# Four norm borders of a two-layer transformer kernel written out by hand, and modulation weights in buffers of their own

## The chip, the core and the metric

The kernel runs on one core of a Trainium2 chip. Its engines are TensorE (PE, matmuls and weight loads), VectorE (DVE), ScalarE (ACT), GpSimd (POOL) and the DMA queues, here SyncE's (SP). Each engine works through a queue of its own in order. The metric is the device time of one execution in microseconds (us), taken as the median of several runs; the profile is one execution of its own.

## The reference

Two layers of a diffusion transformer with d = 1024 work on 256 latent tokens and 256 context tokens. Each layer has three steps: an FFN, a mixer, an FFN. The mixer is a short convolution in layer 0 and grouped-query attention in layer 1. Each step is preceded by an RMS norm with a modulation, and followed by a gated residual addition. Shift, scale and gate (nine vectors a layer, for each of the two streams) are products of silu(c) with a weight matrix. Only the latent stream is returned, so the context drops out after attention of layer 1.

```python
def _rms(t, g):
    y = t * rsqrt(mean(t * t) + eps);  return y * g
def _modulate(t, g, shift, scale):
    return _rms(t, g) * (1 + scale) + shift
def _swiglu(h, w13, w2):
    gte, up = split(h @ w13);  return (silu(gte) * up) @ w2

mod = silu(c) @ mod_w[i] + mod_b[i]            # 3 x (shift, scale, gate)
lat = lat + 0.5 * gate0 * _swiglu(_modulate(lat, g0, shift0, scale0), w13[i, 0], w2[i, 0])
lat = lat + gate1 * mixer(_modulate(lat, g1, shift1, scale1))
lat = lat + 0.5 * gate2 * _swiglu(_modulate(lat, g2, shift2, scale2), w13[i, 1], w2[i, 1])
# the context (ctx, c_ctx) goes through the same steps as long as attention still reads it
```

Here FFN (l, 0) and FFN (l, 1) are the first and second FFN of layer l, and norm (l, j) is the norm ahead of step j.

## The kernel before

**Data.** Features lie on the 128 partitions, in eight "k tiles"; tokens lie along the free axis, 512 columns: 256 latent (stream s = 0) and 256 context (s = 1). `x[:, k, :]` is the residual. Every matmul operand is split into a high part, rounded to the matmul's type, and a low part, the rest (`split`, L110: the high part by ScalarE at L111, the low by VectorE at L112). A product is three matmuls (`mm3`, L131: high x high at L135, high weights x low data at L136, low weights x high data at L137).

**Weights.** `load_raw` (L105) loads 1 MB pages into three buffers with the tag `wr`; the halves of a page are split into `wh` and `wl`.

**FFN** (`ffn`, L689). The 22 tiles of hidden features go in two halves of eleven. In each half some tiles are computed as "plain" units (`w13_mm`: 48 matmuls, over all 512 columns or over the two streams apart), the others as `Pair` units by a Strassen form (`prod`: 84 matmuls of 256 columns, on sums of quarters of the weights, and on sums T1 to T4 of the blocks of h, which `Blocks.sums` makes). `PLAIN` says how many are plain. The pair loop is written out by hand under `manual_schedule` for TensorE, VectorE and ScalarE; elsewhere a scheduler orders the instructions. After eleven tiles, `project` (L495) multiplies by w2: eight tiles of output (m), each a sum over eleven tiles of hidden features. Its start takes in what is left of the last pair: `prev.seven` with the addition `p` (L675), and `last` with `four`, `gate`, `gate_parts`. The conv mixer's and attention's projections use `project` too, over eight tiles.

**Norm borders.** In the projection that ends a step, m = 6 and 7 are computed by streams (`late`): m = 6, 7 for s = 0, and then for s = 1. `finish` (L474) adds gate x product to the residual (L479); `tail_norm` (L429) then squares (L252), accumulates (L255), and, behind m = 7, queues the norm as closures in `pending`, which `flush` runs at chosen places in the code. The norm itself is `rms_sums` (matmuls with ones, L267; root on ScalarE, L272; reciprocal, L276), `rms_rows` (1/rms broadcast over the partitions into PSUM by matmul, L281), and for each k tile and stream: `scaled` (VectorE, x times scale times 1/rms, L289), then on ScalarE the addition of the shift into the high part (L299), on VectorE the low part (L300). A `Blocks` norm also keeps an unsplit copy `hr` (L343) for the sums T1 to T4. `ready` (L493) runs a Sqrt early, which brings ScalarE's function table. Four borders are such: norm (0,1) ahead of the conv mixer, (0,2) ahead of FFN (0,1), (1,0) ahead of FFN (1,0), (1,1) ahead of attention. I call them borders 1 to 4. In borders 1, 3 and 4 the projection sums eleven tiles, in border 2 eight.

**Modulation.** The modulation vectors are made by VectorE in 224 units `junk` (L155), each 128x1024 with its product and sum. Their weights come as 64 pages `modT` of 1 MB through the same `wr` buffers: `open_job` loads a page and queues its four units (or two), `tick(n)` spends n units at a place in the code, `ask_ahead` loads a page early, and `mod_ready` runs what is still missing when a vector is needed.

**The last stage** (L1534 and on) projects FFN (1,1) for the latents alone. For two output tiles at a time it loads three pages: two of `w2l` and one of `w2m`.

Of the kernel before, what the change touches and what calls it, by code (L numbers as in the profile page):

```python
# [24 lines left out]
PLAIN = {(0, 0): 8, (0, 1): 2, (1, 0): 2, (1, 1): NM}  # L25
# [16 lines left out]
def hybrid_kernel(ctx: ExitStack, tc: tile.TileContext, a: dict, out: bass.AP):  # L42
# [62 lines left out]
    def load_raw(src, n=2048):  # L105
        raw = wp.tile([P, 2048], F32, name=nm("wr"), tag="wr", bufs=3)
        nc.sync.dma_start(raw[:, :n], src)
        return raw

# [39 lines left out]
    def mod_unit(l, ch, pair, raw, j, v):  # L149

        mt = mod_tile(l, ch)
        kt = pair * 2 + j
        col = ch * KT + kt
        junk = mp.tile([P, D], BF16, name=nm("junk"), tag="junk", bufs=1)
        nc.vector.tensor_tensor_reduce(  # L155
            out=junk,
            in0=raw[:, j * D : j * D + D],
            in1=scbc[:, v, :],
            scale=1.0,
            scalar=modb[:, l, col : col + 1],  # L160
            op0=ALU.mult,
            op1=ALU.add,
            accum_out=mt[:, kt, v : v + 1],
        )
        done[l, ch] += 1
# [4 lines left out]
    def mod_job(l, ch, pair):  # L170
        mod_tile(l, ch)
        raw = load_raw(a["modT"][l, ch * 4 + pair])
        for j in range(2):
            for v in range(streams(l, ch)):
                mod_unit(l, ch, pair, raw, j, v)

    jobs = [(0, ch, p) for ch in range(2, 9) for p in range(4)]
    jobs += [(1, ch, p) for ch in range(9) for p in range(4)]
# [4 lines left out]
    def open_job():  # L183
        l, ch, pair = jobs.pop(0)
        mod_tile(l, ch)
        raw = load_raw(a["modT"][l, ch * 4 + pair])
        units.extend(
            (l, ch, pair, raw, j, v) for j in range(2) for v in range(streams(l, ch))
        )

    def next_unit():
        if not units:
            open_job()
        with tc.issue_after(begun[-1].ins):
            mod_unit(*units.pop(0))

    def ask_ahead():
        if not units and jobs:
            open_job()
# [59 lines left out]
    def rms_inv(s, parts):  # L259
        return rms_rows(*rms_sums(s, parts))  # L260

    def rms_sums(s, parts):

        pq = psmall("ss")
        for i in range(2):
            for n, t in enumerate(parts):
# [3 lines left out]
                )  # L270
        rs = tp.tile([P, 2], F32, name=nm("rs"), tag="rs")
        nc.scalar.activation(  # L272
            out=rs, in_=pq[:, S : S + 2], func=AF.Sqrt, scale=1.0 / D, bias=eps_t
        )
        ri = tp.tile([P, 2], F32, name=nm("ri"), tag="ri")
        nc.vector.reciprocal(ri, rs)  # L276
        return pq, ri
# [8 lines left out]

    def scaled(s, k, A, ri):
        t = tp.tile([P, S], F32, name=nm("t"), tag="t", bufs=3)
        nc.vector.scalar_tensor_tensor(  # L289
            out=t, in0=x[:, k, s * S : s * S + S], scalar=A[:, k, s : s + 1], in1=ri,  # L290
            op0=ALU.mult, op1=ALU.mult,
        )
        return t

    def norm_k(s, k, h, A, B, ri, keep=None):
        hh, hl = pick(h, k, s * S, s * S + S)
        t = scaled(s, k, A, ri)
        b = B[:, k, s : s + 1]
        nc.scalar.activation(out=hh, in_=t, func=AF.Identity, bias=b)  # L299
        nc.vector.scalar_tensor_tensor(  # L300
            out=hl, in0=t, scalar=b, in1=hh.bitcast(F32), op0=ALU.add, op1=ALU.subtract
        )
        if keep is not None:
            nc.scalar.activation(out=keep, in_=t, func=AF.Identity, bias=b)
# [14 lines left out]

    def pick(h, k, c0, c1):  # L320
        return h.at(k, c0, c1)

    class Blocks:
# [5 lines left out]
        def block(self, s, hf, A, B, ri, fine=False):  # L329
            raw = self.raw[hf, s] = hot("hr", F32)  # L330
            hi, lo = self.t["B", hf, s] = hot("bh"), hot("bl")
            for i in range(4):
                k = 4 * hf + i
                c = slice(i * S, i * S + S)
                t = scaled(s, k, A, ri)
                b = B[:, k, s : s + 1]
                if fine:
                    nc.scalar.activation(out=hi[:, c], in_=t, func=AF.Identity, bias=b)
                    nc.vector.scalar_tensor_tensor(
                        out=lo[:, c], in0=t, scalar=b, in1=hi[:, c].bitcast(F32),  # L340
                        op0=ALU.add, op1=ALU.subtract,
                    )
                nc.scalar.activation(out=raw[:, c], in_=t, func=AF.Identity, bias=b)  # L343
            if not fine:
                split(hi, lo, raw)

        def at(self, k, c0, c1):
            return self.blk(("B", k // 4, c0 // S), k % 4)

        def blk(self, key, k):  # L350
            return tuple(t[:, k * S : k * S + S] for t in self.t[key])

        def sums(self, n):
# [3 lines left out]
            tt = nc.vector.tensor_tensor  # L357

            def keep(key, src):
                hi, lo = self.t[key] = hot("th"), hot("tl")  # L360
                split(hi, lo, src)

            if n == 0:
                tt(out=b11, in0=b12, in1=b11, op=ALU.subtract)
                keep("T1", b11)
            elif n == 1:
                tt(out=b12, in0=b22, in1=b12, op=ALU.add)
                tt(out=b22, in0=b22, in1=b11, op=ALU.add)
                keep("T2", b22)
            else:  # L370
                tt(out=b21, in0=b21, in1=b22, op=ALU.subtract)
                keep("T3", b12)
                keep("T4", b21)
# [48 lines left out]
    pending = []  # L422

    def flush(n=9):
        while pending and n:
            pending.pop(0)()
            n -= 1

    def tail_norm(l, j, h):  # L429

        box = {}

        def tail(m, c0, c1):
            square_add(m, c0, c1)
            if m == KT - 1:
                if not box:
                    box["A"] = scale_of(l, j)
                    box["B"] = mod_ready(l, 3 * j)
                s = c0 // S

                def inv():
                    return rms_inv(s, (accs[s], accs[s, "last"]))

                def rest(part, ri):

                    if isinstance(h, Blocks):
                        h.block(s, part, box["A"], box["B"], ri, fine=s == 0 and part == 0)
                    else:
                        for k in range(4 * part, 4 * part + 4):
                            norm_k(s, k, h, box["A"], box["B"], ri)  # L450

                def both_parts():
                    ri = inv()
                    for part in range(2):
                        rest(part, ri)

                if s == 0:
                    keep = []

                    def one():  # L460
                        keep.append(inv())
                        rest(0, keep[0])

                    pending.append(one)
                    pending.append(lambda: rest(1, keep[0]))
                    if (l, j) == (1, 2):
                        flush()
                else:
                    flush()
                    pending.append(both_parts)  # L470

        return tail

    def finish(m, ps, c0, c1, gate, tail):  # L474
# [12 lines left out]
        if tail:  # L487
            tail(m, c0, c1)
# [6 lines left out]
    def project(ws, src, nk, gate, tail, tot, late, ev, between=()):  # L495

        def products(ps, w, ks, c0, c1):
            for k in ks:
                mm3(ps[:, : c1 - c0], w(k), src(k, c0, c1), k == 0, k == nk - 1)
# [12 lines left out]
        if between:  # L517
            products(p2[0], w2[0], range(nk // 2), 0, tot)
            between[0]()
            products(p2[0], w2[0], range(nk // 2, nk - 2), 0, tot)  # L520
            between[1]()
            products(p2[1], w2[1], range(nk - 2), 0, tot)
            for i in range(nf):
                products(p2[i], w2[i], (nk - 2,), 0, tot)
        else:
            for i in range(nf):
                products(p2[i], w2[i], range(nk - 1), 0, tot)
        for i in range(nf):
            products(p2[i], w2[i], (nk - 1,), 0, tot)
            finish(i, p2[i], 0, tot, gate, tail)  # L530
            tick(ev)

        for m in range(nf, KT - late):
            if tail and tot == S and m == KT - 2:
                ready()
            w = get(m)
            ps = psum("py")
            products(ps, w, range(nk), 0, tot)
            finish(m, ps, 0, tot, gate, tail)
            if m < (KT - late - 1 if tail else KT - 2):  # L540
                tick(ev)
        if late:

            wl = [get(m) for m in (6, 7)]
            if tail:
                ready()
            for s in range(2):
                for i in range(2):
                    ps = psum("py")
# [1271 lines left out]
```

## Time and profile before

| | us |
|---|---|
| runs | 1585.12 to 1589.19, median 1587.78 |
| profiled execution, own time | 1588.48 |
| its span | 1586.3 |
| mean granted clock of TensorE | 0.992 |
| TensorE busy | 1559.8 |
| VectorE busy | 1301.8 |
| ScalarE busy | 731.1 |

The profile names an instruction by its line, its engine, its operation and its tiles (out<-in, buffer numbers left out). A row of groups gives the count, the busy time in us and the mean in ns of one, then the idle time of the engine just before and what ended it. A row of windows gives a stretch of the span in us, its length, and for each engine busy time and number of instructions, then the clock granted to TensorE, the DMA share and GB/s. A row of the chain gives the start, the length and what ran; a row of the timeline the same with the idle time before. Matmuls overlap: a matmul of 256 columns is listed with 0.28 us, but the next one starts 0.12 us later. Vector and scalar instructions overlap by somewhat under 0.1 us.

### The profile page before, as it was taken

To read this page: it belongs to the slowest core of one execution; us is meant where nothing else is said; L and a number is where in the kernel's file an instruction comes from. 1 tells how busy PE (TensorE), PEld (TensorE's weight loads), DVE (VectorE), ACT (ScalarE), POOL (GpSimd) and SP (SyncE) were. 2 spreads that over 40 slices of the span, in tenths; PEclk is the share of its full clock that TensorE was granted. 3 is DMA by queue.
4 is the path that set the end of the run, shared out by engine and by line. 5 is a ranking of instruction groups with operands and counts; after the bars stand their busy time and mean duration, and the time that the engine had idled before them with its cause. 6 is when DMAs were issued, how large, how long until landed. Compare 5 with 4: busy or idle time off the path is not lost.

```text
span 1586.3 us, 25078 instructions
## 1 busy us (share of the span) xinstructions
PE 1559.8 (98%) x10264; PEld 1427.5 (90%) x10264; DVE 1301.8 (82%) x1949; ACT 731.1 (46%) x1189; POOL 34.2 (2%) x28
## 2 busy tenths in 40 slices
PE   8999999999999999999999999999999899999998
PEld 6789899988888899988999899988999789998887
DVE  5787889987988789987997889988997866788654
ACT  4524245524322365522554365523554255775543
POOL 0000000000000000000000000000000002420000
PEclk9999999999999999999999999999999999999999
DMA  9353533255455413345333613355344832256552
GB/s 369 125 201 127 186 127 133 96 185 184 160 187 184 159 55 107 125 172 195 107 133 107 225 54 127 109 192 171 133 160 153 287 127 98 85 194 253 186 195 97
DMA packets 42498, 248.73 MB, mean 157 GB/s; under 512 B 5648, under 2 KB 8208, under 8 KB 18960
## 3 DMA queue, kind: packets, MB, share of 16 engines
q1 hardware_dynamic: 41664, 246.97, 44.1%
q8 instruction: 80, 1.31, 0.3%
q14 instruction: 34, 0.28, 0.1%
q10 hardware_dynamic: 720, 0.17, 0.0%
HBM read 244.77 MB, written 1.05 MB: 155 GB/s over the span
## 4 chain that ended last, share of the span: by engine, by line
PE 84%; DVE 9%; DMA 3%; ACT 3%; issue 1%; POOL 0%; DVEq 0%; ACTq 0%; POOLq 0%
PE py L135 8%; PE py L136 8%; PE py L137 8%; PE p L135 5%; PE p L137 5%; PE p L136 5%; PE q L137 4%; PE py L1534 4%; PE q L135 4%; PE q L136 4%; PE pg L1534 3%; PE pu L1534 3%; DMA wr<-in_modT 2%; DVE wl L611 2%; DVE junk L155 2%; PE pv L137 1%
## 5 line engine op out<-in xcount | busy, mean ns | idle before, releaser
L111 ACT ACTIVATE wh<-wr 128x1024 fp32r<-128x1024 f32 (+1 forms) x228 | 209.1, 936 | 274.2 <-PE py L136 91.4
L155 DVE CUSTOM_DVE_ANT_0 junk<-wr,scbc,modb 128x1024 bf16<-128x1024 f32 x224 | 286.9, 1281 | 30.9 <-DMA wr<-in_modT 28.8
L112 DVE TENSOR_TENSOR wl<-wr,wh 128x1024 fp32r<-128x1024 f32 (+1 forms) x228 | 241.7, 1073 | 64.1 <-ACT wh L111 26.9
L135 PE MATMUL py<-gh,wh 128*128 128x512 f32 (+1 forms) x594 | 219.2, 369 | 4.4 <-ACT wh L111 4.4
L608 ACT ACTIVATE wh<-wr 128x1024 fp32r<-128x1024 f32 x162 | 166.3, 1056 | 115.6 <-DVE wr L631 80.4
L136 PE MATMUL py<-gl,wh 128*128 128x512 f32 (+1 forms) x594 | 218.5, 368 | 0.0
L137 PE MATMUL py<-gh,wl 128*128 128x512 f32 (+1 forms) x594 | 218.2, 367 | 0.0
L611 DVE TENSOR_TENSOR wl<-wr,wh 128x1024 fp32r<-128x1024 f32 x162 | 192.9, 1217 | 22.6 <-ACT wh L608 22.6
L135 PEld LDWEIGHTS py<-gh,wh 128*128 128x128 f32 x594 | 113.5, 191 | 22.1 <-ACT wh L111 4.6
L137 PEld LDWEIGHTS py<-gh,wl 128*128 128x128 f32 x594 | 113.3, 191 | 18.2
L136 PEld LDWEIGHTS py<-gl,wh 128*128 128x128 f32 x594 | 113.3, 191 | 17.5
L136 PE MATMUL p<-tl,wh 128*128 128x256 f32 x432 | 122.3, 283 | 0.0
L137 PE MATMUL p<-th,wl 128*128 128x256 f32 x432 | 122.3, 283 | 0.0
L135 PE MATMUL p<-th,wh 128*128 128x256 f32 x432 | 122.2, 283 | 0.0
L137 PE MATMUL q<-bh,wl 128*128 128x256 f32 x320 | 90.8, 284 | 1.2 <-DVE wl L611 1.2
L135 PE MATMUL q<-bh,wh 128*128 128x256 f32 x320 | 90.7, 283 | 0.5 <-ACT wh L608 0.5
L136 PE MATMUL q<-bl,wh 128*128 128x256 f32 x320 | 90.6, 283 | 0.0
L136 PEld LDWEIGHTS p<-tl,wh 128*128 128x128 f32 x432 | 82.9, 192 | 0.2
L135 PEld LDWEIGHTS p<-th,wh 128*128 128x128 f32 x432 | 82.9, 192 | 0.2
L137 PEld LDWEIGHTS p<-th,wl 128*128 128x128 f32 x432 | 82.9, 192 | 0.0
L626 DVE TENSOR_TENSOR wr<-wr 128x1024 f32<-128x1024 f32 x54 | 66.1, 1224 | 1.6
L137 PE MATMUL q<-th,wl 128*128 128x256 f32 x216 | 61.8, 286 | 1.2 <-DVE wl L611 1.2
(326 smaller groups left out, 4109.1 us busy)
## 6 DMA issues: line engine op xcount, KB each, us to landing
wr<-in_w SPq DMA_DIRECT2D x85, 1024.0 KB, 4.8
wr<-in_modT SPq DMA_DIRECT2D x64, 1024.0 KB, 4.8
wr<-in_w2h SPq DMA_DIRECT2D x48, 704.0 KB, 4.1
mr<-in_mod SPq DMA_DIRECT2D x16, 512.0 KB, 9.0
wr<-in_cw_cx SPq DMA_DIRECT2D x8, 1024.0 KB, 4.8
wr<-in_w2l SPq DMA_DIRECT2D x8, 1024.0 KB, 4.8
wr<-in_cw_b SPq DMA_DIRECT2D x4, 1024.0 KB, 5.0
wr<-in_cw_out SPq DMA_DIRECT2D x4, 1024.0 KB, 5.1
```

Of the source, the lines that this page charges most:

```text
L111: nc.scalar.activation(out=hi, in_=src, func=AF.Copy)
L112: nc.vector.tensor_tensor(out=lo, in0=src, in1=hi.bitcast(F32), op=ALU.subtract)
L135: nc.tensor.matmul(ps, wh, mh, start=first, stop=False, **kw)
L136: nc.tensor.matmul(ps, wh, ml, start=False, stop=False, **kw)
L137: nc.tensor.matmul(ps, wl, mh, start=False, stop=last, **kw)
L155: nc.vector.tensor_tensor_reduce(out=junk, in0=raw[:, j * D : j * D + D], in1=scbc[:, v, :], scale=1.0, scalar=modb[:, l, col : col + 1], ...
L608: nc.scalar.activation(out=self.shaped(g, 0), in_=self.part(g), func=AF.Copy)
L611: nc.vector.tensor_tensor(out=self.shaped(g, 1), in0=self.part(g), in1=self.shaped(g, 0).bitcast(F32), op=ALU.subtract,)
L626: tt(out=by_two(raw[:, :1024]), in0=a21.unsqueeze(1).to_broadcast([P, 2, T2]), in1=by_two(raw)[:, :, :T2], op=ALU.subtract,)
L1534: nc.tensor.matmul(p[:, :n], w(j, k)[part], m(k)[:, :n], start=not part and k == 0, stop=part == 1 and k == nk - 1, skip_group_check=True,)
```

## The change

- Weight pages get two `wr` buffers in place of three. Modulation weights get two buffers `wm` of their own, each half as large, and are loaded in 128 halves of 512 KB; `ask_ahead` keeps two halves in hand and is called around each unit.
- FFN (0,1) and FFN (1,0), which begin at borders 2 and 3, have three plain units and eight pairs in the first half, in place of two and nine.
- The norm at borders 1 to 4 is a class `Border`. ScalarE makes x times scale (`scaled`) into `hr`, for k tiles 0 to 3 from m = 4 on, for 4 and 5 at the opening, and for 6 and 7 behind each square; when 1/rms is there, VectorE multiplies four k tiles at once (`mult`, 128x1024); `hi` (ScalarE) and `lo` (VectorE) split each k tile with its shift, and `shift` adds it in place for the block sums.
- The opening of each border (`open_border`: the four blocks of m = 6 and 7, the norm of s = 0 and the first weight splits) and the start of the next stage are written out for TensorE, VectorE and ScalarE. `part_mm` orders the matmuls by part (high x high, low weights, low data), so that they begin on the high parts of four k tiles. Modulation vectors of the norm are made ready when `Border` is made, at m = 4.
- `Halves` is a weight page whose two halves are split when asked; `Post` is the plain unit's silu, gate and split, step by step; `Blocks.sub`, `hi`, `lo` replace `Blocks.sums`.

```diff
-PLAIN = {(0, 0): 8, (0, 1): 2, (1, 0): 2, (1, 1): NM}
+PLAIN = {(0, 0): 8, (0, 1): 3, (1, 0): 3, (1, 1): NM}
...
-        raw = wp.tile([P, 2048], F32, name=nm("wr"), tag="wr", bufs=3)
+        raw = wp.tile([P, 2048], F32, name=nm("wr"), tag="wr", bufs=2)
...
+    def mod_raw():
+        return wp.tile([P, D], F32, name=nm("wm"), tag="wm", bufs=2)
...
+    def ask_ahead():
+        while jobs and len({u[2] for u in units}) < 2:
+            l, ch, kt = jobs.pop(0)
+            mod_tile(l, ch)
+            raw = mod_raw()
+            src = a["modT"][l, ch * 4 + kt // 2]
+            nc.sync.dma_start(raw, src[:, kt % 2 * D : kt % 2 * D + D])
+            units.extend((l, ch, kt, raw, v) for v in range(streams(l, ch)))
...
+    class Border:
+        def scaled(self, k, s):
+            nc.scalar.activation(
+                out=self.part(k, s), in_=x[:, k, s * S : s * S + S], func=AF.Identity,
+                scale=self.A[:, k, s : s + 1],
+            )
...
+        def mult(self, hf, s):
+            t = self.raw[hf, s].rearrange("p (k t) -> p k t", k=4)
+            nc.vector.tensor_tensor(
+                out=t, in0=t, in1=self.ss[s][:, :S].unsqueeze(1).to_broadcast([P, 4, S]),
+                op=ALU.mult,
+            )
...
+    def open_border(bd, v, early=False):
+        short = bd.nk == KT
+        mid = 5 if short else 6
+        def whi(i):
+            v[i][0].hi(v[i][1])
+        def wlo(i):
+            v[i][0].lo(v[i][1])
+        ready()
+        for s in range(2):
+            for k in (4, 5):
+                bd.scaled(k, s)
+        bd.late(0, 0)
+        if short:
+            for i in range(2):
+                whi(i)
+                wlo(i)
+        tick(2)
+        bd.fin(0, 0)
+        bd.square(0, 0)
+        bd.late(0, 1)
+        if not short:
+            tick(1)
+        bd.add(0)
+        bd.fin(1, 0)
+        bd.square(1, 0)
+        bd.late(1, 0, range(mid))
+        if not short:
+            whi(0)
+        bd.sums(0)
+        bd.root(0)
+        bd.late(1, 0, range(mid, bd.nk))
+        bd.inv(0)
+        bd.rows(0)
+        if not short:
+            wlo(0)
+            whi(1)
+        bd.fin(0, 1)
+        bd.late(1, 1)
+        bd.mult(0, 0)
+        bd.square(0, 1)
+        bd.hi(low, 0)
+        if not short:
+            wlo(1)
+        bd.add(1)
+        bd.mult(1, 0)
+        if early:
+            whi(2)
+        bd.fin(1, 1)
+        bd.hi((4, 5), 0)
+        bd.square(1, 1)
+        bd.hi((6, 7), 0)
+        bd.lo(low, 0)
+        return whi, wlo
...
-        for m in range(nf, KT - late):
-            if tail and tot == S and m == KT - 2:
-                ready()
+        for m in range(nf, 6 if norm else KT):
...
+            if norm and m == 4:
+                b = Border(*norm)
+                for k in range(4):
+                    for s in range(2):
+                        b.scaled(k, s)
...
+    def border_ffn(l, b, h, bd):
+        w = [Halves(a["w13"][l, b, i]) for i in range(2)]
+        whi, wlo = open_border(bd, [(w[i], j) for i in range(2) for j in range(2)])
+        w.append(Halves(a["w13"][l, b, 2]))
...
+        g = groups(0, 0)
+        for n in range(2):
+            part_mm(g, low, n, 0, h, True, False)
+        whi(2)
+        bd.sums(1)
+        bd.root(1)
+        part_mm(g, low, 2, 0, h, False, False)
+        bd.lo(high, 0)
+        bd.inv(1)
+        for n in range(2):
+            part_mm(g, high, n, 0, h, False, False)
+        whi(3)
+        bd.rows(1)
+        part_mm(g, high, 2, 0, h, False, True)
+        wlo(2)
+        wlo(3)
...
```

More of the change, by code (lines that the diff above doesn't have):

```diff
@@ L327, in __init__, with slot @@
             self.raw, self.t = {}, {}
[L329 to L345, printed above, removed]
+        def slot(self, k, s):
+            key = ("B", 0, s) if k < 4 else ("H", k // 2)
+            if key not in self.t:
+                self.t[key] = hot("bh"), hot("bl")
+            return self.at(k, s * S, s * S + S)
```

584 lines of the change are left out of this document (374 added, 210 removed).

## The prediction

> **What bounds the kernel now.** I read the page's totals and its chain first.
>
> ```profile
> span 1586.3 us, 25078 instructions
> PE 1559.8 (98%) x10264; PEld 1427.5 (90%) x10264; DVE 1301.8 (82%) x1949; ACT 731.1 (46%) x1189; POOL 34.2 (2%) x28
> PE 84%; DVE 9%; DMA 3%; ACT 3%; issue 1%; POOL 0%; DVEq 0%; ACTq 0%; POOLq 0%
> ```
>
> TensorE is the bound: 98% busy and 84% of the chain that ended last. What can be won without removing matmuls is the rest of the chain, VectorE's 9% above all. Where it lies I read from windows over the four norm borders, beside two undisturbed stretches.
>
> ```profile
> core 0: us, PE busy (x) PEld busy (x) DVE busy (x) ACT busy (x) POOL busy (x), PEclk, DMA share, GB/s
> 640.00:660.00 20.00, 20.00 (x169) 20.00 (x168) 18.14 (x24) 11.30 (x18) 0.00 (x0) 1.00 0.40 135
> 540.00:555.00 15.00, 15.00 (x67) 12.40 (x67) 7.41 (x10) 4.90 (x7) 0.00 (x0) 1.00 0.22 88
> 380.00:400.00 20.00, 16.80 (x122) 16.72 (x121) 17.46 (x37) 9.77 (x20) 0.00 (x0) 0.83 0.44 158
> 565.00:610.00 45.00, 43.19 (x351) 42.15 (x350) 41.85 (x59) 31.84 (x52) 0.00 (x0) 1.00 0.19 62
> 920.00:955.00 35.00, 32.24 (x263) 31.39 (x262) 32.79 (x42) 24.18 (x37) 0.00 (x0) 1.00 0.18 61
> 1260.00:1295.00 35.00, 28.42 (x200) 27.87 (x200) 23.05 (x48) 17.20 (x30) 0.00 (x0) 0.85 0.44 168
> 385.00:390.00 5.00, 2.12 (x10) 2.12 (x11) 4.77 (x10) 2.20 (x6) 0.00 (x0) 0.65 0.00 0
> 390.00:395.00 5.00, 5.00 (x31) 5.00 (x31) 3.51 (x5) 0.00 (x0) 0.00 (x0) 0.66 0.80 279
> 1260.00:1265.00 5.00, 0.64 (x4) 0.44 (x4) 4.17 (x10) 3.33 (x5) 0.00 (x0) 0.88 0.74 274
> 1265.00:1270.00 5.00, 5.00 (x25) 5.00 (x25) 2.17 (x5) 0.57 (x2) 0.00 (x0) 0.50 0.82 306
> ```
>
> The counts matter more than busy time, since a matmul that waits or runs at half clock still counts as busy. In the pair loop (first row) 169 matmuls of 256 columns take 20 us, 0.118 us each; matmuls of 512 columns (second row) take 15/67 = 0.224 us. The borders run 256 columns. At 0.118 us border 1 (380 to 400, before the conv mixer) should hold 169 matmuls and holds 122: 47 x 0.118 = 5.5 us lost. Border 2 (565 to 610, conv to FFN) lacks 380 - 351 = 29, 3.4 us; border 3 (920 to 955) 296 - 263 = 33, 3.9 us; border 4 (1260 to 1295, before attention) 296 - 200 = 96, 11.3 us. Together 24.1 us: what the change can win at most. Part of it is the granted clock: TensorE idles 2.9 us in 385 to 390 and then has 0.65 to 0.66; after 4.4 us of idling at 1260 it has 0.50, and 25 matmuls in 5 us where 42 fit.
>
> The chain at border 4 shows what started that idling.
>
> ```profile
> 1253.98 7.19 DMA wr<-in_modT
> 1261.22 0.44 issue
> 1261.66 1.28 DVE junk L155
> 1262.95 0.62 DVE acc L255
> 1263.70 0.83 ACT wh L111
> 1264.58 0.58 PE py L135
> ```
>
> A modulation page waited for its turn in the weights' buffers; the unit that reads it (`junk`, L155) held VectorE's queue, and the accumulation and the weight split behind it held TensorE.
>
> **The change part by part.** Durations of one instruction are from the groups by shape.
>
> ```profile
> L608 ACT ACTIVATE wh<-wr 128x1024 fp32r<-128x1024 f32 x162 | 166.3, 1056 | 115.6 <-DVE wr L631 80.4 <-PE pg L136 14.3 <-DMA wr<-in_w 10.4
> L299 ACT ACTIVATE hh<-t,mod 128x256 fp32r<-128x256 f32 x32 | 14.2, 497 | 9.7 <-DVE t L289 9.7
> L155 DVE CUSTOM_DVE_ANT_0 junk<-wr,scbc,modb 128x1024 bf16<-128x1024 f32 x224 | 286.9, 1281 | 30.9 <-DMA wr<-in_modT 28.8
> L611 DVE TENSOR_TENSOR wl<-wr,wh 128x1024 fp32r<-128x1024 f32 x162 | 192.9, 1217 | 22.6 <-ACT wh L608 22.6
> L479 DVE SCALAR_TENSOR_TENSOR x<-py,G,x 128x256 f32<-128x256 f32 x96 | 42.0, 478 | 18.4 <-PE py L137 18.1
> L289 DVE SCALAR_TENSOR_TENSOR t<-x,A,ss 128x256 f32<-128x256 f32 x64 | 27.4, 477 | 5.7 <-PE ss L281 5.7
> L300 DVE SCALAR_TENSOR_TENSOR hl<-t,mod,hh 128x256 fp32r<-128x256 f32 x32 | 14.0, 483 | 0.8 <-ACT hh L299 0.7
> L255 DVE TENSOR_TENSOR acc<-acc,sq 128x256 f32<-128x256 f32 x14 | 5.9, 422 | 3.4 <-ACT sq L252 3.2
> L252 ACT ACTIVATE sq<-x 128x256 f32<-128x256 f32 x23 | 9.5, 411 | 23.0 <-DVE x L479 19.9 <-DVE x L1547 3.0
> L255 DVE TENSOR_TENSOR acc<-acc,sq 128x512 f32<-128x512 f32 x20 | 13.7, 687 | 1.5 <-ACT sq L252 1.5
> L252 ACT ACTIVATE sq<-x 128x512 f32<-128x512 f32 x20 | 12.7, 632 | 32.3 <-DVE x L479 32.1
> ```
>
> *1/rms by four k tiles.* The 64 multiplications at L289 (16 a border) become 4 a border of 128x1024. No row has that operation with one operand from PSUM; L611, an operation on two tensors of that size, is nearest at 1.22, against 4 x 0.48 for what it replaces: I take 1.22, between 1.2 and 1.9. A border saves 16 x 0.48 - 4 x 1.22 = 2.8 us of VectorE and gains 16 `scaled` of some 0.45 on ScalarE, made early beside the projection (46% busy). None is on the path by itself; what counts is when the first operands are ready.
>
> *Borders 1, 3, 4* (eleven k tiles). After the change four `late` blocks of 33 matmuls, 33 x 0.118 = 3.9 us each, run while the norm is made. The sums of squares come after block two and 18 matmuls, at 9.9 us; from there 15 matmuls and block four give 5.7 us of cover. In that time go the sum, root, reciprocal and broadcast (some 1.6 us), `mult` (1.2) and four `hi` (4 x 0.50 = 2.0): 4.8 us, with `fin` (0.48) between. So the first matmuls of the next stage are about due; I take 1.3 us of loss at border 1, where the schedule has a junk unit (1.28) ahead of the `lo` that TensorE needs second, 0.8 at border 3 and 1.0 at border 4, where the modulation page no longer waits for a weight buffer. Bounds: 0 each, and their losses now without border 4's start, 5.5, 3.9 and 11.3 - 4.4 - 2.4.
>
> *Border 2* (eight k tiles) has blocks of 24 x 0.118 = 2.8 us, and TensorE comes to the sums at 2 x 2.8 + 15 x 0.118 = 7.4 us. The written order on VectorE is: two splits `wlo`, two junk units, and only then `fin(0,0)`. The splits wait for `whi` on ScalarE, queued behind `ready` and four `scaled`: x of m=5 at about 0.9, its square at 1.6, accumulated at 2.3, `ready` 2.6, `scaled` to 4.1, `whi` to 5.1 and 6.1, `wlo` to 7.3, two junks to 9.8, `fin(0,0)` to 10.2, add and `fin(1,0)` to 11.4, square to 11.9. TensorE idles 11.9 - 7.4 = 4.4 us. After an idling of just this length, in the row from 1265, 17 matmuls of 42 were lost in 5 us (2.0 us), the clock still 0.50 at its end; I take 2.4. Border 2 then costs 6.8 us, twice what it costs now. Bounds: 0.8, as at border 3, and 8.
>
> [...]
>
> *A third plain unit* in the FFNs behind borders 2 and 3 in place of a Strassen pair: 48 x 0.118 + 24 x 0.224 = 11.0 us against 84 x 0.118 = 9.9, so +1.1 each, on TensorE: +2.3. This has one answer.
>
> *Modulation pages in own buffers, half as large; weights with two buffers for three.*
>
> ```profile
> wr<-in_modT SPq DMA_DIRECT2D x64, 1024.0 KB, 4.8
> wr<-in_w2h SPq DMA_DIRECT2D x48, 704.0 KB, 4.1
> DVE junk L155 <- DMA wr<-in_modT: 28.8, 18, 3.8
> ```
>
> The 64 pages become 128, issued on SP's queue, which is only DMA issues. By 704 KB in 4.1 and 1024 KB in 4.8, 512 KB should take about 3.7 us; two pages (two streams of 1.28 each, so 5.1 us of junk work) are kept ahead, which covers it. VectorE's 28.8 us of waits for pages mostly go; they are slack except at border 4. [...]
>
> What the weights lose is a buffer. In the pair loop a weight is asked for two pairs ahead and freed once split; with 9.9 us a pair and 4.8 a load half the time is slack, and I take 0 there, in attention and in the plain stages; the bound is B below. In the last stage not:
>
> ```profile
> 1536.60 0.33 SPq L107 DMA_DIRECT2D wr<-in_w2l  x1
> 1543.71 0.33 SPq L107 DMA_DIRECT2D wr<-in_w2m  x1
> ```
>
> With two buffers the third load (`w2m`) waits for the `lo` of the first; I work out that it lands some 2.8 us late, against 11 matmuls of 512 or 256 columns (2.5 us at most) put before its use. 0.3 each at three of four places, 1.0 in all; bounds 0 and 3 x 2.8.
>
> *The six project starts.* Since units are now kept ready, the scheduler puts up to four junks between the last pair's `sg` and its `p` (L675) where there were none to two.
>
> ```profile
> 318.89 0.69 DVE L684 TENSOR_TENSOR gm<-sg,p 128x512 f32<-128x512 f32 x1 [0.51 <-PE p L137]
> 320.28 0.69 DVE L112 TENSOR_TENSOR gl<-gm,gh 128x512 fp32r<-128x512 f32 x1 [0.70 <-ACT gh L111]
> 323.75 0.43 DVE L675 TENSOR_TENSOR p<-p,gm 128x256 f32<-128x256 f32 x1 [2.78 <-PE p L137]
> 326.30 0.28 PE L135 MATMUL p<-th,w4h 128*128 128x256 f32 x1
> ```
>
> VectorE's gaps here are 0.51 + 0.70 + 2.78 = 4.0 us, and `p` is done 2.1 us before TensorE uses it. Four junks are 5.1 us, 1.1 over the gaps, within the 2.1; but the TensorE order moves this use one to three matmuls earlier. I take 0.5 at five starts, 2.5; bounds 0 and 3 each.
>
> **Sum.** Lost after: 1.3 + 6.8 + 0.8 + 1.0 + 2.3 + 2.5 + 1.0 = 15.7 us; before: 24.1. The profiled execution (1588.5 us, of it 1586.3 span) comes to 1580.1; the median shown is 0.7 lower than it, so 1579.4.
>
> **The rivals.** *A, better:* border 2 doesn't stall, because the square comes before `ready` or the junks are late. Then 6.8 becomes 0.8: 1573.4. Against it, VectorE's queue runs in written order.
>
> *B, slower:* at the project starts the junks wait for their pages, and `p` and the splits of the projection's weights wait behind them in VectorE's queue, as at border 4 now. The longest wait for a page is 3.8 us and the pages are asked for through one queue with the weights, whose two buffers hold it up: a load that waits for a buffer holds back the page behind it. At 3 us for each of six starts, 18 in place of 2.5: 1594.9. It costs more than the change wins from (8.4 + 2.5)/6 = 1.8 us a start. Against it: at most starts the pages are in own buffers and asked for early.
>
> *C, no change:* the gain is given back. VectorE is the bound behind borders 2 and 3 (41.85 of 45 us, 32.79 of 35 busy), so border 3 keeps its 3.9 (+3.1), and the wait of 4.4 us that border 4 loses returns at a projection whose page is late: 1579.4 + 7.5 = 1586.9. Against it: VectorE has 2.8 us less a border.
>
> **How the numbers follow.** The forecast has 0.44, A 0.12, C 0.20, B 0.24. 0.3% (4.8 us) is about what a measurement of this kernel tells from no change: faster is forecast and A, 0.56; same C, 0.20; slower B, 0.24. The range goes from 1570, border 2 without a stall and the other borders at their lower bounds (3 us under A), to 1595, B at its price. The forecast's own is 1575 to 1584: border 2 from 0.8 upwards, the starts at 0 to 1.5.
>
> **What would show it.** Border windows: TensorE short of under 12 matmuls at borders 1, 3 and 4; at border 2 an idling of about 4 us ahead of `ss`, waiting for a square, then a clock near 0.5. Waits: junk for its page well under 28.8. Junks between `sg` and `p` at project starts, the `p` matmuls waiting under 1 us. In the last stage a wait for `w2m` under 1 us. I am wrong if border 2 has no gap, if splits wait for loads in the pair loop (the two buffers), or if page waits stand ahead of `p`.

## The result

The changed kernel takes 1576.18 us (median, 1575.5 to 1577.45) against 1588.49 us for the kernel before on the same chip: the ratio is 0.9927, 95% interval 0.991 to 0.9944. The profiled execution's span is 1573.9 us, 12.4 less than before. The forecast was 1579.4 with a range of 1570 to 1595; the time lies in it, and the gain is half as large again as forecast.

The page after, its totals and its chain:

```profile
span 1573.9 us, 25256 instructions
PE 1557.0 (99%) x10240; PEld 1422.7 (90%) x10240; DVE 1286.5 (82%) x1905; ACT 755.2 (48%) x1261; POOL 34.2 (2%) x28
PE 94%; DVE 2%; ACT 1%; DMA 1%; issue 0%; POOL 0%; ACTq 0%; DVEq 0%; POOLq 0%
```

VectorE's part of the chain fell from 9% to 2%, though its busy time fell by 15 us only: it is late less often, not much less busy. Windows over the four borders after, in the columns of the prediction's:

```profile
375.00:395.00 20.00, 19.99 (x167) 19.66 (x167) 16.80 (x28) 12.46 (x26) 0.00 (x0) 1.00 0.34 122
555.00:600.00 45.00, 40.85 (x321) 40.57 (x321) 37.91 (x54) 29.91 (x58) 0.00 (x0) 0.92 0.24 83
908.00:943.00 35.00, 35.00 (x296) 35.00 (x296) 28.61 (x44) 27.12 (x55) 0.00 (x0) 1.00 0.27 92
1255.00:1285.00 30.00, 30.00 (x255) 30.00 (x253) 22.09 (x37) 21.60 (x43) 0.00 (x0) 1.00 0.35 116
```

At 0.118 us a matmul, border 1 is 2 matmuls short of 169, borders 3 and 4 not at all, and border 2 is 380 - 321 = 59 short: 7.0 us, twice what it lost before. Three borders are closed, and one is worse.

To compare kernels I use one finer measure, the time between the starts of two neighbouring matmuls less the steady 0.120 us (256 columns) or 0.227 (512), summed over a place. In us lost by TensorE:

| | border 1 | border 2 | after it | border 3 | after it | border 4 | last stage |
|---|---|---|---|---|---|---|---|
| before | 5.8 | 1.8 | 1.5 | 1.2 | 2.8 | 11.4 | 0.9 |
| changed | 0.4 | 6.9 | 1.3 | -0.1 | 1.3 | -0.1 | 2.3 |
| own buffers alone | 2.5 | 1.8 | 1.5 | 1.2 | 2.8 | 11.7 | 2.5 |
| early vectors alone | 5.1 | 1.8 | 1.5 | 1.2 | 2.8 | 10.1 | 0.9 |
| own buffers, early vectors | 3.9 | 1.8 | 1.5 | 1.2 | 2.8 | 9.5 | 2.5 |
| changed, pages in the weights' buffers | 2.3 | 7.2 | 4.6 | 6.9 | 3.2 | -0.1 | 0.9 |
| changed, splits late at border 2 | 0.4 | 1.4 | 1.3 | -0.1 | 1.3 | -0.1 | 2.0 |

"After it" is the rest of the start of the FFN, up to 70 us behind the sums. Each row is one traced execution. Changed against before, the columns give 12.0 - 25.4 = -13.4; the third plain units add +2.3 by matmul counts (72 fewer of 256 columns, 48 more of 512: -8.6 + 10.9); small places elsewhere give -1.5. Together -12.6, against 12.4 between the spans.

### The profile page after: what moved, and what is told of

The parts are those of the page before. It is cut to its first block, busy times and chain, and to the rows that moved or that the text cites. A ratio compares the mean times of both kernels' runs of the same rounds, so it can differ in the third digit from the quotient of the medians.

```text
span 1573.9 us, 25256 instructions
## 1 busy us (share of the span) xinstructions
PE 1557.0 (99%) x10240; PEld 1422.7 (90%) x10240; DVE 1286.5 (82%) x1905; ACT 755.2 (48%) x1261; POOL 34.2 (2%) x28
## 4 chain that ended last, share of the span: by engine, by line
PE 94%; DVE 2%; ACT 1%; DMA 1%; issue 0%; POOL 0%; ACTq 0%; DVEq 0%; POOLq 0%
PE py L138 9%; PE py L140 9%; PE py L139 9%; PE p L138 6%; PE p L140 6%; PE p L139 6%; PE q L140 5%; PE q L138 4%; PE q L139 4%; PE pu L1817 3%; PE pg L1817 3%; PE py L1817 2%; PE pg L522 2%; PE pu L522 2%; PE pg L1202 1%; PE pv L138 1%
## 5 line engine op out<-in xcount | busy, mean ns | idle before, releaser
L114 ACT ACTIVATE wh<-wr 128x1024 fp32r<-128x1024 f32 (+1 forms) x210 | 190.7, 926 | 248.4 <-PE py L139 128.1
L157 DVE CUSTOM_DVE_ANT_0 junk<-wm,scbc,modb 128x1024 bf16<-128x1024 f32 x224 | 286.9, 1281 | 24.6 <-DMA wm<-in_modT 22.7
L115 DVE TENSOR_TENSOR wl<-wr,wh 128x1024 fp32r<-128x1024 f32 (+1 forms) x210 | 220.1, 1060 | 71.8 <-ACT wh L114 29.7
L747 DVE TENSOR_TENSOR wl<-wr,wh 128x1024 fp32r<-128x1024 f32 x156 | 186.1, 1218 | 27.7 <-ACT wh L744 27.7
L744 ACT ACTIVATE wh<-wr 128x1024 fp32r<-128x1024 f32 x156 | 160.5, 1056 | 100.5 <-DVE wr L767 59.0
L140 PE MATMUL p<-th,wl 128*128 128x256 f32 x416 | 117.7, 283 | 0.0
L139 PE MATMUL p<-tl,wh 128*128 128x256 f32 x416 | 117.7, 283 | 0.0
L138 PE MATMUL q<-bh,wh 128*128 128x256 f32 x304 | 86.0, 283 | 0.0
L140 PE MATMUL q<-bh,wl 128*128 128x256 f32 x304 | 86.0, 283 | 0.0
L114 ACT ACTIVATE gh<-gm 128x512 fp32r<-128x512 f32 x60 | 37.8, 631 | 52.1 <-DVE gm L820 47.7
```

The costliest lines, as they stand in the source:

```text
L114: nc.scalar.activation(out=hi, in_=src, func=AF.Copy)
L115: nc.vector.tensor_tensor(out=lo, in0=src, in1=hi.bitcast(F32), op=ALU.subtract)
L138: nc.tensor.matmul(ps, wh, mh, start=first, stop=False, **kw)
L139: nc.tensor.matmul(ps, wh, ml, start=False, stop=False, **kw)
L140: nc.tensor.matmul(ps, wl, mh, start=False, stop=last, **kw)
L157: nc.vector.tensor_tensor_reduce(out=junk, in0=raw, in1=scbc[:, v, :], scale=1.0, scalar=modb[:, l, col : col + 1], op0=ALU.mult, op1=ALU.add,
```

## The experiments

**What makes border 2's stall.** The timeline of VectorE in the changed kernel at border 2 (start, length, what, idle before), with TensorE's first matmul of the sums:

```profile
555.49 2.36 DVE L503 TENSOR_TENSOR wl<-wr,wh 128x1024 fp32r<-128x1024 f32 x2 [2.82 <-ACT wh L498]
557.77 1.28 DVE L157 CUSTOM_DVE_ANT_0 junk<-wm,scbc,modb 128x1024 bf16<-128x1024 f32 x1
559.09 1.28 DVE L157 CUSTOM_DVE_ANT_0 junk<-wm,scbc,modb 128x1024 bf16<-128x1024 f32 x1
560.30 0.48 DVE L429 SCALAR_TENSOR_TENSOR x<-py,mod,x 128x256 f32<-128x256 f32 x1
561.26 0.42 DVE L442 TENSOR_TENSOR acc<-acc,sq 128x256 f32<-128x256 f32 x1 [0.48 <-ACT sq L437]
561.61 0.48 DVE L429 SCALAR_TENSOR_TENSOR x<-py,mod,x 128x256 f32<-128x256 f32 x1
561.74 0.58 PE L256 MATMUL ss<-ones,acc 128*128 128x1 f32 x2 [3.89 <-DVE acc L442]
```

This is the queue that the prediction wrote out: 2.8 us of waiting for `whi`, two splits, two units, and only then the first `fin`. Two runs part the splits from the units. The first:

```diff
         if short:
             for i in range(2):
                 whi(i)
                 wlo(i)
-        tick(2)
+        else:
+            tick(2)
...
         bd.square(1, 0)
+        if short:
+            tick(2)
```

> The changed kernel, but in the opening of border 2 alone the two junk units stand behind the second square instead of ahead of the first fin. If the stall of border 2 (4.4 us of idling, then the half clock, 6.9 us lost in all) is made by what stands ahead of fin in VectorE's written order, two units of 1.24 us less shorten the idling to about 1.9 us and the time by about 3.5 us against the changed kernel (1576.2 to about 1572.7). If it is made by the residual of m = 5 or by ready on ScalarE, nothing changes.

Measured: 1574.49 us, ratio to before 0.9909 (0.9894 to 0.9923); border 2 loses 5.2 us in place of 6.9. The idling got shorter as expected. The gain, 1.7 us by the medians and at border 2 in the trace, is half of what I expected, and the interval overlaps that of the changed kernel. The windows say why it is small. First the changed kernel, then this one, two microseconds each:

```profile
559.00:561.00 2.00, 0.00 (x0) 0.00 (x0) 1.75 (x5) 0.18 (x1) 0.00 (x0) 0.90 0.77 287
561.00:563.00 2.00, 1.00 (x4) 0.92 (x5) 0.82 (x2) 1.44 (x4) 0.00 (x0) 0.50 0.99 360
563.00:565.00 2.00, 2.00 (x10) 2.00 (x11) 0.17 (x1) 0.26 (x1) 0.00 (x0) 0.50 0.26 107
```
```profile
557.00:559.00 2.00, 1.36 (x12) 1.16 (x10) 1.75 (x3) 0.21 (x1) 0.00 (x0) 1.00 0.00 0
559.00:561.00 2.00, 0.82 (x4) 0.74 (x5) 1.77 (x3) 1.42 (x4) 0.00 (x0) 0.87 0.80 246
561.00:563.00 2.00, 2.00 (x10) 2.00 (x11) 1.62 (x5) 0.26 (x1) 0.00 (x0) 0.50 0.68 279
563.00:565.00 2.00, 2.00 (x12) 2.00 (x11) 0.48 (x1) 0.32 (x1) 0.00 (x0) 0.50 0.54 174
```

TensorE is idle for only 0.64 and then 1.18 us in the first two windows of this run, and still falls to half clock (0.50 in 561 to 565). The penalty was not in proportion to the gap: with 1.8 us of idling here and 4.2 in the changed kernel the half clock stood for the same 6.8 us.

The second run moves the splits instead:

```diff
-        if short:
-            for i in range(2):
-                whi(i)
-                wlo(i)
         tick(2)
...
         bd.square(1, 0)
+        if short:
+            for i in range(2):
+                whi(i)
+                wlo(i)
```

> The changed kernel, but in the opening of border 2 the two weight splits stand behind the second square, and the two junk units stay ahead of the first fin, as at the long borders. By my theory the junks fit in the first block (2.5 of 2.8 us), the sums are ready when TensorE comes to them, and the idling of 4.4 us goes; the norm's chain behind the sums is then the next limit (1 to 1.5 us). 1576.2 less 5.5, about 1570.7. By the rival that border 2 is bound by the length of the chain, whatever its order, the stall moves behind the sums and the time stays.

Measured: 1569.35 us, ratio 0.9879 (0.9866 to 0.9893). Border 2 loses 1.4 us, nearly all of it in one gap of 1.36 us ahead of the broadcast of 1/rms, and the clock stays at full:

```profile
555.00:560.00 5.00, 3.92 (x34) 3.71 (x33) 3.11 (x5) 2.86 (x5) 0.00 (x0) 1.00 0.01 3
560.00:565.00 5.00, 5.00 (x42) 4.97 (x43) 4.38 (x8) 3.95 (x11) 0.00 (x0) 1.00 0.58 210
```

So the written order made the stall, the splits above all: they wait 2.82 us for ScalarE, and all that stands behind them waits too (the first `fin` starts at 560.30 in the changed kernel).

**Is it the buffers, or the written borders?** By the traces of the two kernels alone one could say that the written borders win nothing (border 1 and 3 won what border 2 and the plain units cost) and that the modulation pages' buffers are the whole gain. Two runs have one of the two each, the first the borders and the second the buffers:

```diff
 (changed kernel, undone)
-        raw = wp.tile([P, 2048], F32, name=nm("wr"), tag="wr", bufs=2)
+        raw = wp.tile([P, 2048], F32, name=nm("wr"), tag="wr", bufs=3)
...
-    jobs = [(0, ch, k) for ch in range(2, 9) for k in range(KT)]
+    jobs = [(0, ch, p) for ch in range(2, 9) for p in range(4)]
...
+        raw = load_raw(a["modT"][l, ch * 4 + pair])
```

```diff
 (kernel before, with this alone)
-        raw = wp.tile([P, 2048], F32, name=nm("wr"), tag="wr", bufs=3)
+        raw = wp.tile([P, 2048], F32, name=nm("wr"), tag="wr", bufs=2)
...
+    def mod_raw():
+        return wp.tile([P, D], F32, name=nm("wm"), tag="wm", bufs=2)
...
+        while jobs and len({u[2] for u in units}) < 2:
```

> The changed kernel with the modulation pages as before: 64 of 1 MB through the weights' buffers, three of them. If written-out borders are what wins, the time stays near 1576 (the last stage gains 1.2 back). If the buffers of their own are what wins, a page again waits for a weight buffer ahead of border 4 and costs what it cost there, 4.5 us of idling and 2.9 of half clock: about 1583.

> The kernel before with the modulation pages' own buffers alone (halves of 512 KB, two weight buffers), no written border and no third plain unit. By the traces of both kernels: border 4's wait for a page (7.4 us with its half clock) and the 1.0 us in a pair at 804 go, the last stage loses 1.2: 1588.5 less 7.2, about 1581.3. By the rival that the buffers are the whole gain, 1576; by the rival that the loss of a weight buffer costs in the pair loop without the written border, 1585 or more.

Measured: the written borders without the buffers take 1591.58 us, ratio 1.0019 (1.0007 to 1.0031), slower than before. The buffers without the written borders take 1586.28 us, ratio 0.9981 (0.9968 to 0.9993). One part costs 3 (2.3 of it are, by count, the third plain units, which came with the borders), the other wins 2, both together win 12. The traced execution of the first lies 3 us under its median and that of the second 2 us over, so the table's rows don't add up to these medians. Both of my expectations were wrong. For the buffers alone a rival's number came out (1585 or more), but not by its mechanism, waits in the pair loop; the table shows where the time is: with the pages in the weights' buffers border 4 is closed all the same, but borders 1 and 3 are not; with the buffers alone border 4 stays open, at 11.7 us in place of 11.4. Border 3 of the former, VectorE's timeline and SP's:

```profile
918.58 1.28 DVE L155 CUSTOM_DVE_ANT_0 junk<-wr,scbc,modb 128x1024 bf16<-128x1024 f32 x1 [7.05 <-DMA wr<-in_modT]
919.79 0.48 DVE L437 SCALAR_TENSOR_TENSOR x<-py,G,x 128x256 f32<-128x256 f32 x1
911.56 0.33 SPq L107 DMA_DIRECT2D wr<-in_modT  x1
```

The opening's `tick(2)` is in VectorE's written order ahead of `fin`; its page could be asked for only at 911.56, behind a weight. VectorE stood for 7.05 us with the norm behind it. In the changed kernel the same operation (there L429) waits for TensorE alone:

```profile
907.53 0.48 DVE L429 SCALAR_TENSOR_TENSOR x<-py,G,x 128x256 f32<-128x256 f32 x1 [1.69 <-PE py L140]
```

So the buffers let units be put inside borders 1 and 3 at little cost. By themselves they also win 3.3 us at border 1, and 1.9 at three places in front of `p` (see below); at border 4 they win nothing, and in the last stage they lose 1.6.

Border 4 with the buffers alone, VectorE's timeline:

```profile
1265.40 0.48 DVE L471 SCALAR_TENSOR_TENSOR x<-py,G,x 128x256 f32<-128x256 f32 x1
1269.09 1.28 DVE L157 CUSTOM_DVE_ANT_0 junk<-wm,scbc,modb 128x1024 bf16<-128x1024 f32 x1 [3.21 <-DMA wm<-in_modT]
1270.42 1.28 DVE L157 CUSTOM_DVE_ANT_0 junk<-wm,scbc,modb 128x1024 bf16<-128x1024 f32 x1
1271.63 0.16 DVE L268 RECIPROCAL ri<-rs 128x2 f32<-128x2 f32 x1
```

Units still stand ahead of the reciprocal, and their pages come late even with buffers of their own. Three more runs asked whether the place of the demand does it. In the kernel before, with the buffers and without:

```diff
             square_add(m, c0, c1)
+            if m == 4 and (l, j) != (1, 2):
+                box["A"] = scale_of(l, j)
+                box["B"] = mod_ready(l, 3 * j)
             if m == KT - 1:
```

> The kernel before with two parts of the change: the modulation pages' own buffers, and the norm's shift and scale made ready at m = 4 instead of behind m = 7; no written border. With the buffers alone border 4 still lost 11 us, because six or so units were asked for behind m = 7 and their pages came one by one in the middle of the norm. If it is the place of that demand, border 4 falls to 4 us or less and the time by some 7 us against the buffers alone (1586.3), to about 1579. If the pages come too slowly wherever they are asked for, the loss moves to m = 4 and the time stays.

> The kernel before with one part of the change: the norm's shift and scale made ready at m = 4, pages still of 1 MB through the weights' three buffers. If the place of the demand is enough by itself, border 4 gives 7 us, about 1581. If the pages must also have buffers of their own, a page still waits there for a weight's buffer and the time stays within 2 us of 1588.4.

And in the changed kernel, the shift asked for in the opening:

```diff
-            self.A, self.B = scale_of(l, j), mod_ready(l, 3 * j)
+            self.A, self.need = scale_of(l, j), (l, 3 * j)
...
         ready()
+        bd.B = mod_ready(*bd.need)
```

> The changed kernel, but the shift vector of the norm (B) is made ready in the border's opening, behind ready, instead of at m = 4; scale stays at m = 4. The units still missing then stand in VectorE's written order ahead of the first fin. If the early demand is a part of the gain, border 4 loses 4 us or more (its units are the ones that are behind) and the time rises from 1576.2 to 1580 or more. If two pages in hand cover it, the same within 1 us.

Measured: 1583.89 us, ratio 0.9972 (0.996 to 0.9984); 1588.34 us, ratio 1.0003 (0.999 to 1.0015); and 1576.64 us, ratio 0.9934 (0.992 to 0.9947), the same as the changed kernel. The place of the demand is a small part at most: border 4 still loses 9.5 and 10.1 us with it, and nothing is lost without it. What does differ is how many units are done early. By the first sums of border 3, 165 of the 224 are done in the kernel before and in the three runs with the buffers, the early vectors or both, and 174 in the two kernels that close border 4 (the changed one, and the one with its pages in the weights' buffers). The written openings spend units at borders 1 to 3 (`tick(2)`, `tick(1)`, and one in the first pair). From 15 us ahead of border 4's first sums to 25 us behind them, 3 units run in the kernel before, 8 with the buffers alone, 4 with the early vectors alone and 8 with both, against 0 and 2.

Such a debt of units can account for the first part of border 4's loss at most, up to the second stream's sums: 5.9 to 7.4 us in the four kernels that leave it open. The other 3.6 to 5.1 us follow at the second stream's sums, where no unit stands. In each of the four TensorE waits there for the square of the last tile, in the kernel before:

```profile
1283.25 0.38 PE L267 MATMUL ss<-ones,sq 128*128 128x1 f32 x2 [1.70 <-ACT sq L252]
```

That tile's residual addition stands behind `t` and `hl` of the first stream's norm in VectorE's queue (it starts at 1281.98, its last matmul at 1280.57), and the half clock follows (0.50 in 1285 to 1287). In the changed kernel the second sums don't wait. No run moves the units alone or this order alone, so both causes are inferred from the traces. What is shown is that neither the buffers nor the early demand closes border 4, and that the written borders, with the third plain units, close it with either kind of buffers.

**Smaller parts.** 1/rms by one k tile in place of four:

```diff
-            nc.vector.tensor_tensor(
-                out=t, in0=t, in1=self.ss[s][:, :S].unsqueeze(1).to_broadcast([P, 4, S]),
-                op=ALU.mult,
-            )
+            for i in range(4):
+                t = self.part(4 * hf + i, s)
+                nc.vector.tensor_tensor(out=t, in0=t, in1=self.ss[s][:, :S], op=ALU.mult)
```

> The changed kernel, but 1/rms multiplies one k tile at a time: 16 operations of 128x256 a border in place of 4 of 128x1024. If one large operation is what made the norm short, each border that TensorE reaches late pays 0.4 to 0.5 us more for the first four k tiles, 1 to 2 us over the four, 1577.2 to 1578.2. If the gain is only in the order, the same within 0.4 us, since four small ones take about 1.6 us against 1.2.

Measured: 1576.19 us, ratio 0.9922 (0.99 to 0.9943), no difference to the changed kernel. The prices, first of the changed kernel and then of this one:

```profile
L458 DVE TENSOR_TENSOR hr<-hr,ss 128x1024 f32<-128x1024 f32 x16 | 19.2, 1218 | 0.8 <-PE ss L276 0.4
```
```profile
L459 DVE TENSOR_TENSOR hr<-hr,ss 128x256 f32<-128x256 f32 x64 | 22.3, 418 | 0.5 <-PE ss L276 0.4
```

The large operation saves 3 us of VectorE in the whole kernel. Only borders 1 and 2 show it on TensorE, +0.2 and +0.5.

The first matmuls behind a border k tile by k tile:

```diff
+        if n:
+            return
         for k in ks:
...
+                for q in range(3):
+                    nc.tensor.matmul(
+                        ps, w[q == 1], hl if q == 2 else hh,
```

> The changed kernel, but the first matmuls behind the borders run k tile by k tile, all three products of each, instead of first all those with the high part of four k tiles. TensorE then needs the first low part at once, which VectorE makes behind the last fin: about 0.9 us more at each border, 3.6 in all, about 1579.8. If the low parts are ready anyway, the same.

Measured: 1581.87 us, ratio 0.9953 (0.9936 to 0.997): 5.7 us over the changed kernel. Border 1 loses 3.2 more, border 2 1.2, borders 3 and 4 1.0 each. At border 1 TensorE waits for the low part, which VectorE makes behind a unit (382.69 to 383.89):

```profile
384.43 0.43 PE L525 MATMUL pv<-hl,wh 128*128 128x256 f32 x1 [1.94 <-DVE hl L473]
```

One page asked ahead in place of two:

```diff
-        while jobs and len({u[2] for u in units}) < 2:
+        while jobs and len({u[2] for u in units}) < 1:
```

> The changed kernel with only one modulation page asked ahead instead of two (a page is then two units, 2.6 us of work, against about 3.7 us for its load). If the second page in hand is what keeps units from holding VectorE's queue, waits for pages grow by 64 times 1 us and some of it, 2 to 5 us, gets into TensorE's path. If such waits lie in VectorE's idle time, the same within 1 us.

Measured: 1576.17 us, ratio 0.992 (0.9901 to 0.9938), the same. VectorE's waits for pages are 23.9 us against 22.7. The second page in hand is worth nothing that can be measured; buffers of their own are, since the written borders take 1576 us with them and 1592 without.

**A faster version.** In the last stage the changed kernel waits for `w2m`, as foreseen. The order of the loads was changed, on top of the late splits:

```diff
-                load_w(a["w2l"][t, 0]), load_w(a["w2l"][t, 1]), load_w(a["w2m"][t], 12 * P)
-            )
+            first = load_w(a["w2l"][t, 0])
+            mid = load_w(a["w2m"][t], 12 * P)
+            box[t] = first, load_w(a["w2l"][t, 1]), mid
```

> The changed kernel with both mends: the splits of border 2 behind the second square, and in the last stage the page w2m loaded second instead of third, so that the page that waits for a buffer is the one used last. Against the splits alone the three waits for w2m there (about 0.5 to 0.9 us each, 1.2 more in all than before) go: about 1.3 us less, 1569.4. If the wait only moves to the second w2l page, the same as with the splits alone, 1570.7.

Measured: 1569.41 us, ratio 0.9875 (0.9856 to 0.9894). In the trace the last stage's loss falls from 2.0 to 0.3 us, but the median is that of the late splits alone: a gain of this size isn't shown in the time. Then the unit in the first pair:

```diff
                         if prev:
-                            tick(PER_PAIR)
+                            if not bd or i > i1:
+                                tick(PER_PAIR)
```

> The kernel with both mends, and no modulation unit in the first pair behind borders 2 and 3. There the changed kernel loses 1.0 and 1.2 us where TensorE waits for a weight's low part that stands behind T4 and such a unit in VectorE's queue. If the unit is the cause, both go: 1569.4 less 2.3, about 1567.1. If VectorE is behind by more than the one unit, half of it remains.

Measured: 1566.21 us, ratio 0.987 (0.9856 to 0.9885). The losses after borders 2 and 3 fall from 1.3 each to 0.4 and 0.1. The interval overlaps that of the run before, so the step by itself rests on the trace. With both mends and this one the kernel is 10 us faster than the changed kernel by the medians, and border 2 is 346 matmuls long in the window where the changed kernel has 321:

```profile
555.00:600.00 45.00, 43.92 (x346) 42.72 (x345) 37.26 (x52) 31.56 (x59) 0.00 (x0) 1.00 0.19 71
```

## Why the prediction was right, and where it was not

*Direction and place* held: TensorE was the bound, and the gain was in the borders. The forecast said 8.4 us, the spans show 12.4. That the time lies near the forecast is in part luck: terms were wrong in both directions.

*Border 2* was right in its mechanism and its size: 4.4 us of idling forecast, 4.2 between two matmuls measured; 6.8 in all forecast, 6.9 or 7.0 measured. The late splits confirm it. The 1.3 us behind it are in no term.

*The other borders* were sized too carefully: 1.3, 0.8 and 1.0 forecast, 0.4 and nothing measured. The working counted 4.8 us of chain plus `fin` against 5.7 of cover, and then charged a loss that this sum didn't contain (at border 1 for a unit ahead of the low part). That is 2.7 us too much. But the first pairs behind borders 2 and 3 lose 1.3 us each, which no term held, and which the kernel before lost inside the windows that the prediction counted. Over the same places the borders lose 9.7 us, where 9.9 were forecast: the sum came out by two errors that cancel.

*Border 4's cause* was wrong. The prediction read the chain's wait of 7.2 us for a page as a wait for a weight's buffer, and let the pages' own buffers remove it with its half clock. The run with the buffers alone loses 11.7 us there, no less than the 11.4 before; the written borders without the buffers lose nothing. The step that failed is the one that read the start of border 4's loss as a matter of buffers. What the runs put in its place is the written order; how much of that is a debt of units paid earlier stays open. The prediction looked at each part's gain by itself, and the parts don't add: -2 and +3 make -12.

*Waits in front of `p`* were put at nothing: "they are slack except at border 4". In the kernel before three of them were not slack. Near 813, 1005 and 1166 us a unit waited for its page with `p` behind it, and TensorE lost 1.0, 0.4 and 0.5 us:

```profile
811.80 1.28 DVE L155 CUSTOM_DVE_ANT_0 junk<-wr,scbc,modb 128x1024 bf16<-128x1024 f32 x1 [2.74 <-DMA wr<-in_modT]
813.50 0.39 PE L135 MATMUL p<-th,w4h 128*128 128x256 f32 x1 [0.77 <-DVE p L675]
```

These losses are gone in the changed kernel and with the buffers alone, and remain with the early vectors alone. They and a wait at 1427 us (0.8) are 2.7 us of the 4 us by which the gain is larger than forecast; the project starts (below) are 1.4.

*VectorE's waits for pages* were to fall "well under 28.8". They did not:

```profile
DVE junk L157 <- DMA wm<-in_modT: 22.7, 22, 3.3
wm<-in_modT SPq DMA_DIRECT2D x128, 512.0 KB, 4.2
```

They still happen, mostly where nothing urgent stands behind them. Half a page takes 4.2 us, not the 3.7 that was worked out; that is more than one page's two units (2.6 us) cover.

*Third plain units:* +2.3 by count, right. *Last stage:* +1.0 forecast, +1.4 in the trace, and the wait is the one named. *Project starts:* 2.5 us forecast at five places; two of the six show a loss, 0.5 and 0.6 us by the starts of matmuls. Their waits are for `p`:

```profile
327.05 0.39 PE L138 MATMUL p<-th,w4h 128*128 128x256 f32 x1 [0.27 <-DVE p L811]
1214.58 0.39 PE L138 MATMUL p<-th,w4h 128*128 128x256 f32 x1 [0.33 <-DVE p L811]
```

The second shows a sign that the prediction had named as one of being wrong, page waits in front of `p` (0.71 and then 1.07 us, and 0.31 at the first):

```profile
1211.28 1.29 DVE L157 CUSTOM_DVE_ANT_0 junk<-wm,scbc,modb 128x1024 bf16<-128x1024 f32 x1 [1.07 <-DMA wm<-in_modT]
```

So rival B's mechanism was there, at 1.1 us at most and not at 18. The other sign, splits that wait for loads in the pair loop, was not: these waits fell from 16.6 to 7.4 us. B's mechanism was large in another kernel, though: with the pages in the weights' buffers a unit held up `fin` for 7 us, and that kernel was slower than before by 3 us. B was right in what it feared and wrong in the place. *Rival A* would have been the kernel with late splits. *Rival C* had one true piece: VectorE is late in the first pair after borders 2 and 3, 1.3 us each, not foreseen in the sum.

## What to carry to other kernels

In an order written out by hand, a wait costs what stands behind it in the queue, so an operation that waits for another engine (here two weight splits) belongs behind the short ones that the critical engine needs next: border 2 lost 6.9 us with the splits ahead of the first `fin`, waiting 2.82 us, and 1.4 with them behind the second square. Background work that is put inside a tight place must have its data there, in buffers that the foreground can't hold up: with the pages in the weights' buffers a unit stood for 7.05 us at border 3, which lost 6.9 us, and with buffers of their own nothing. Parts of a change that serve each other must be tried together before one is judged: here one part alone was slower and the other hardly faster.

## What the runs showed of the hardware

The half clock came after gaps of different length, and it did not last less with the shorter gap. In the changed kernel it began when TensorE had idled for 2.7 us (557.86 to 560.58), with the late units after 1.7 us of idling in two pieces (558.36 to 560.47, with one pair of short matmuls between); the late splits' gap, 1.1 us of idling in the window of 555 to 560, left the clock at 1.00. In the first two the half clock stood for the same 6.8 us, here the changed kernel and then the late units:

```profile
560.58:567.41 6.83, 5.41 (x24) 5.33 (x25) 2.03 (x6) 2.59 (x7) 0.00 (x0) 0.50 0.42 158
560.47:567.30 6.83, 6.74 (x31) 6.74 (x32) 4.92 (x9) 2.54 (x8) 0.00 (x0) 0.50 0.50 190
```

With the late units the two gaps cost 2.1 us and the clock 3.1 of the 5.2 lost, so there the clock cost more than the gaps. Shortening the idling from 4.2 to 1.8 us won 1.7 us.

A transfer of half the size was not much shorter: the pages of 512 KB in the changed kernel took 4.2 us from issue to landing (median of 128), those of 1024 KB in the kernel before 4.8 (median of 64).
